# Second column pair of the MLP's down projection by seven products in four blocks of a layer instead of three

## The chip, the cores and the metric

The kernel runs on one core of a Trainium2 chip. Its engines work side by side, each with a queue of its own: TensorE (PE, with PEld for the load of its weights) multiplies matrices into PSUM banks, VectorE (DVE) and ScalarE (ACT) work element by element, GpSimd (POOL) and SyncE (SP) here mostly start transfers. Semaphores order them. The metric is the time of one execution in microseconds on the device, as a median of several runs; three runs of the kernel before gave 2193.33 (2192.96 to 2195.0).

## What is computed

A trunk of two decoder layers on 256 tokens of width 2048 in float32. Each layer normalises, runs an attention mixer (two head types in layer 0, sparse attention in layer 1) and adds the result, then normalises again and runs an MLP. The change is in the MLP alone:

```python
def sq_relu_mlp(h, w_up, w_down):
    return jnp.square(jax.nn.relu(h @ w_up)) @ w_down      # 2048 -> 8192 -> 2048

for layer in range(DEPTH):                                 # DEPTH = 2
    hn = rms_norm(h, ln_mix_g[layer])
    h = h + mixer(hn)                                      # even or odd
    hn = rms_norm(h, ln_mlp_g[layer])
    h = h + sq_relu_mlp(hn, w_mlp_up[layer], w_mlp_down[layer])
```

## The kernel before

**Products in three parts.** Every float32 product is made of three matmuls: both operands are split into a high part (a rounded copy, by ScalarE, line 280) and a low part (the value minus the copy, by VectorE, line 283), and high x high, high x low and low x high are summed in PSUM. A weight therefore costs a transfer, a ScalarE copy and a VectorE subtraction before TensorE can use it.

**Units.** The work of TensorE is one list of units, written in `units`; `run` (line 291) walks it. A unit has 1024 columns of weights to split. The split of a unit is issued while TensorE's unit three places ahead of it is issued, and there are four buffers (`wh`, `wl`) for split weights, so ScalarE can begin a split only when TensorE has finished the unit four places back. A plain unit (`a_units`, line 339) has 12 matmuls of 512 columns, lines 366 to 368 and 379. A unit of a seven-product pair has 6, lines 989 to 991.

**The MLP.** The 8192 hidden columns are cut into eight blocks of 1024. `up_units(b)` makes block b of the hidden layer with 16 plain units (two halves g of 512 columns, eight units each). Then comes a chain of small steps for each half: out of PSUM by transposes (line 443), turned over partitions by DMAs (line 449), relu and square on ScalarE, and split into high and low parts in `big` (lines 908 and 910). There is one place for the hidden parts of blocks 0 to 6, so block b may be written only when all of block b - 1 has been used (`used`, line 1010).

**The down projection of a block** has four column blocks of 512, taken as two pairs: c = 0 (columns 0 to 1023) and c = 1 (1024 to 2047). A plain pair (`pair_units`, line 1057) has 8 plain units. A pair by seven products (`seven_units`, line 937) has the tokens, the hidden rows and the columns cut in two each and makes the 2x2 by 2x2 block product with seven products in place of eight: x0, z0, x1, y0, x2, y1, x3, in this order, each of two units (a and b here). For this it needs sums of weights and sums of tokens:

- Sums of weights are made in four stage buffers of 1 MB (`Stage`, line 215). A stage is loaded by SP (line 229) or made from another one by an addition: on VectorE for x1, x2 and x3 (line 239, two halves of 1024 columns each), by a DMA that POOL starts and that adds as it writes for y1 (line 237). A VectorE addition is issued four units after the split that frees its place, or at the latest with the split that needs it.
- Sums of tokens are made once per block by `token_sums` (line 918): four rounds of a VectorE operation (line 929), a ScalarE copy (932) and a VectorE operation (934). They start when the sums of the block before have been used (`passed`, "sums") and when both hidden halves are there. x1, y0, x2 and y1 use them.

x0, z0 and x3 use the hidden parts themselves. The results of six of the seven products are added to the residual `xs` at once (line 1000); z0's product stays in a bank over the blocks and is added at the last block that has one (`ends`).

`WIDE = (1, 3, 5)` says in which blocks the second pair goes by seven products too. The first pair does in blocks 0 to 6; block 7 is plain throughout. So a layer has ten such pairs.

**What sets the order.** The list of units is written by hand: after the 16 units of `up_units(0)` come groups (the loop at line 1074), in each of which the units of the seven-product pairs are woven into plain units at the places `at`: `mine[0], others[0], mine[1]`, then the other plain units up to the next place. A spacing of one means one plain unit between the two units of a product and none behind them; a spacing of two, one more behind. The groups before:

| group | plain units | seven-product units |
| --- | --- | --- |
| 1 | up 1, pair c = 1 of block 0 (24) | block 0 c = 0 (14) |
| 2 | up 2, up 3, pair of block 2 (40) | block 1 c = 0 and 1, block 2 c = 0 (42) |
| 3 | up 4, up 5, pair of block 4 (40) | block 3 c = 0 and 1, block 4 c = 0 (42) |
| 4 | up 6, up 7, pair of block 6 (40) | block 5 c = 0 and 1, block 6 c = 0 (42) |

In groups 2 to 4 the spacing is two but for four places: z0 to x1 in all three pairs, and y0 to x2 in the second. Block 7's 16 plain units end the layer.

The chains of small steps (hidden parts, token sums) are generators that `Background` hands out: after every three matmuls comes a slot (line 331), in which up to two waiting steps are issued; a step says by `yield` how many slots the next one must wait. Where a unit needs the result of a chain that isn't done, `need` (line 143) runs slots until it is, so that all remaining steps are issued at once ahead of that unit. A unit of 12 matmuls has four slots, one of 6 has two.

Of the kernel before, what the change touches and what calls it, by code (L numbers as in the profile page):

```python
# [148 lines left out]
def trunk_kernel(ctx: ExitStack, tc: tile.TileContext, x, w_up, w_down, even_w_in, even_w_out,  # L149
# [303 lines left out]
    class Norm:  # L453
# [83 lines left out]
        def need(self, ks):  # L537
            if self is norms[0] and max(ks) < 2:
                return
            for n in {k // 4 for k in ks}:  # L540
                bg.need(self.tasks[n])
# [327 lines left out]
    def mlp(layer, norm, nxt):  # L869
        up, down = w_up[layer], w_down[layer]  # L870
        NBLK = DFF // 1024
        WIDE = (1, 3, 5)

        def hid(b):


            return big[:, 0:8] if b < NBLK - 1 else big[:, 8:16]
# [59 lines left out]
        def seven_units(b, c):  # L937

            def w(r, n):
                at = c * 1024 + n * 512
                return down[b * 1024 + r * 512:b * 1024 + r * 512 + 512, at:at + 512].rearrange("(k p) c -> p k c", p=128)

            turn = len(kept)
            places = summed + [smw[:, 0:2048]]
            bx, by, bz, bw = (places[(i - turn) % 4] for i in range(4))
            old = kept.get(turn - 1)
            final = c == 1 or b not in WIDE

            def gone(f):

                return f if turn else lambda i: current[0] >= start[0] and all(t.done for t in norm.tasks.values())

            x0 = Stage(bx, gone(lambda i: old["x1"].have[i] and old["y1"].have[i]), src=w(0, 0))
            z0 = Stage(bz, gone(lambda i: old["y1"].used[i]), src=w(1, 0))
            w0 = Stage(bw, gone(lambda i: old["z0"].used[i] and old["x3"].have[i]), src=w(0, 1))
            y0 = Stage(by, gone(lambda i: old["x3"].used[i]), src=w(1, 1))
            x1 = Stage(bx, lambda i: x0.used[i] and w0.have[i], add=w0.buf, prev=x0)
            x2 = Stage(bx, lambda i: x1.used[i] and y0.have[i], add=by, prev=x1)  # L960
            y1 = Stage(by, lambda i: y0.used[i] and x2.have[i] and w0.have[i], add=w0.buf, prev=y0, far=True)
            x3 = Stage(bx, lambda i: x2.used[i] and z0.have[i], add=bz, prev=x2)
            kept[turn] = dict(x1=x1, x3=x3, y1=y1, z0=z0)

            def hx(j0, half):
                return lambda j, part: hid(b)[:, j0 + j, part, half * 128:half * 128 + 128]

            def sx(i):
                return lambda j, part: xsum[:, part, i, j]

            h0 = lambda: [heads["hid", b, 0]]
            hd = lambda: [heads["hid", b, g] for g in range(2)]
            sm = lambda: [heads["sum", layer, b]]
            P, Q, R = bank[0], bank[1 + 2 * c], bank[2]
            ends = b == (NBLK - 2, WIDE[-1])[c]
            out_ = []

            for n, (st, lhs, need, o, new, half, col, neg) in enumerate((
                    (x0, hx(0, 0), h0, P, True, 0, 0, 0), (z0, hx(4, 0), hd, Q, b == c, 0, 0, 0),
                    (x1, sx(0), sm, R, True, 1, 1, 0), (y0, sx(3), sm, R, False, 0, 1, 0),  # L980
                    (x2, sx(1), sm, P, False, 0, 1, 1), (y1, sx(2), sm, P, False, 1, 1, 1),
                    (x3, hx(4, 1), hd, P, False, 1, 0, 0))):
                for i in range(2):
                    def gen(u, n=n, i=i, lhs=lhs, need=need, o=o, new=new, half=half, col=col, neg=neg):
                        bg.need(*need())
                        h, lo = (t[u % NHL].rearrange("p (j c) -> p j c", j=2) for t in (wh, wl))
                        for j in range(2):
                            jj = 2 * i + j
                            nc.tensor.matmul(o, lhs(jj, 0), h[:, j], start=new and jj == 0, stop=False, skip_group_check=True)  # L989
                            nc.tensor.matmul(o, lhs(jj, 0), lo[:, j], start=False, stop=False, skip_group_check=True)  # L990
                            nc.tensor.matmul(o, lhs(jj, 1), h[:, j], start=False, stop=jj == 3 and (n != 1 or ends), skip_group_check=True)  # L991
                            if jj == 3 and n == 0 and c == 1:
                                passed.add(("low", b))
                            if jj == 3 and (n != 1 or ends):
                                at = (2 * c + col) * 512
                                xd = xs[:, half, at:at + 512]
                                f = 2 * neg + half
                                if b == 0 and n == 0:
                                    bg.need(norm.rtask)
                                nc.vector.scalar_tensor_tensor(xd, o, norm.r2[:, f:f + 1], xd, op0=ALU.mult, op1=ALU.add)  # L1000
                                if final:
                                    passed.update({("sums", b)} if n == 5 else {("seven", b)} if n == 6 else ())
                            yield

                    out_.append((st, i * 1024, 1024, gen, True))
            return out_
# [3 lines left out]
        def used(b, g):  # L1010
# [3 lines left out]
            if b == NBLK - 1:  # L1014
                return ("sums", b - 1) in passed
            need_ = {("low", b - 1)} if g == 0 else {("seven", b - 1)} if b - 1 in WIDE else {("seven", b - 1), ("eight", b - 1)}
            return need_ <= passed
# [4 lines left out]
        def taken(f, *a):  # L1022
            at = len(units)
            f(*a)
            got = units[at:]
            del units[at:]
            return got
# [43 lines left out]

        start[0] = len(units) + 5
        up_units(0)
        for b in (1, *range(2, NBLK, 2)):
            if b > 1:
                plain_ = taken(up_units, b) + taken(up_units, b + 1) + taken(pair_units, b)
                seven = seven_units(b - 1, 0) + seven_units(b - 1, 1) + seven_units(b, 0)
            else:
                plain_ = taken(up_units, b) + taken(pair_units, b - 1)
                seven = seven_units(b - 1, 0)  # L1080


            m = len(seven) // 2
            if b == 1:
                at = [1, 7, 10, 13, 16, 19, 22]
            else:
                at = [2]
                for i in range(m - 1):
                    at.append(at[-1] + (1 if i in (1, 8, 10, 15) else 2))
            units.extend(plain_[:at[0]])  # L1090
            for i, (a, e) in enumerate(zip(at, at[1:] + [len(plain_)])):
                mine, others = seven[2 * i:2 * i + 2], plain_[a:e]
                units.extend([mine[0], others[0], mine[1]] + others[1:])
# [5 lines left out]

    out_proj(even_w_out, even_ready, norms[1], [(n, a, a + 8) for a in (0, 8) for n in range(NB)], 3)  # L1100
    mlp(0, norms[1], norms[2])


# [226 lines left out]

    out_proj(odd_w_out, odd_ready, norms[3], [(n, 0, 8) for n in range(NB)] + [(n, a, a + 4) for a in (8, 12) for n in range(3)] + [(3, 8, 16)], 0)
    mlp(1, norms[3], None)
    run()

# [52 lines left out]
```

## Time and profile before

| what | value |
| --- | --- |
| median of three runs | 2193.33 us |
| profiled execution, its own time | 2191.8 us |
| its span | 2190.0 us |
| granted clock of TensorE | 1.000 |
| busy: PE, PEld, DVE, ACT | 100%, 83%, 77%, 57% |
| HBM read | 410.52 MB |

The span is that of the instructions of one execution; its time is 1.8 us longer. A busy TensorE says little by itself, because neighbouring matmuls overlap; the waits of TensorE and the chain of work that ended last show whether it sets the time. Row form in the timeline: start in us, duration in us, engine, line, operation, written tile <- read tiles, shape, count, and in brackets the idle time ahead of it with what ended it. Layer 0's MLP lies between 442.5 and 1112.5 us of the span; layer 1's MLP is the last 670 us.

### The profile page before, as it was taken

To read this page: it belongs to the slowest core of one execution; us is meant where nothing else is said; L and a number is where in the kernel's file an instruction comes from. 1 tells how busy PE (TensorE), PEld (TensorE's weight loads), DVE (VectorE), ACT (ScalarE), POOL (GpSimd) and SP (SyncE) were. 2 spreads that over 40 slices of the span, in tenths; PEclk is the share of its full clock that TensorE was granted. 3 is DMA by queue.
4 is the path that set the end of the run, shared out by engine and by line. 5 is a ranking of instruction groups with operands and counts; after the bars stand their busy time and mean duration, and the time that the engine had idled before them with its cause. 6 is when DMAs were issued, how large, how long until landed. Compare 5 with 4: busy or idle time off the path is not lost.

```text
span 2190.0 us, 27524 instructions
## 1 busy us (share of the span) xinstructions
PE 2183.5 (100%) x9965; PEld 1808.6 (83%) x9965; DVE 1695.2 (77%) x2241; ACT 1243.7 (57%) x1563; POOL 76.4 (3%) x68
## 2 busy tenths in 40 slices
PE   9999999999999999999999999999999999999999
PEld 7788888888888888888888888888888888888887
DVE  5676766668989989989764676766689899899895
ACT  5555555455556656656643556555455665665663
POOL 0000000000000000000000000000000000000000
PEclk9999999999999999999999999999999999999999
DMA  7655656587677777777666664535776867867864
GB/s 271 193 190 172 191 187 202 173 285 217 216 239 233 230 243 224 241 240 225 193 196 198 223 197 136 161 109 178 244 241 180 282 203 219 280 198 232 269 203 154
DMA packets 287751, 463.73 MB, mean 212 GB/s; under 512 B 25344, under 2 KB 81920, under 8 KB 287616
## 3 DMA queue, kind: packets, MB, share of 16 engines
q1 hardware_dynamic: 280848, 439.89, 61.2%
q0 software_dynamic: 5760, 20.97, 5.2%
q8 instruction: 78, 1.28, 0.2%
q10 hardware_dynamic: 1008, 1.12, 0.2%
q14 instruction: 57, 0.47, 0.1%
HBM read 410.52 MB, written 2.10 MB: 188 GB/s over the span
## 4 chain that ended last, share of the span: by engine, by line
PE 97%; DVE 2%; DMA 1%; ACT 0%; issue 0%; SPq 0%; POOL 0%; DVEq 0%; ACTq 0%
PE bank L379 48%; PE bank L366 8%; PE bank L368 8%; PE bank L367 8%; PE bank L990 6%; PE bank L991 6%; PE bank L989 6%; PE bank L691 1%; PE bank L723 1%; PE bank L718 1%; PE bank L399 1%; DVE wl L283 1%; PE bank L400 1%; PE bank L398 1%; PE bank L1161 0%; DMA raw<-in_odd_w_in 0%
## 5 line engine op out<-in xcount | busy, mean ns | idle before, releaser
L283 DVE TENSOR_TENSOR wl<-raw,wh 128x1024 fp32r<-128x1024 f32 (+2 forms) x611 | 741.4, 1217 | 308.4 <-ACT wh L280 304.8
L280 ACT ACTIVATE wh<-raw 128x1024 fp32r<-128x1024 f32 (+2 forms) x611 | 642.8, 1056 | 555.0 <-PE bank L379 316.5
L379 PE MATMUL bank<-wh,xT 128*128 128x512 f32 x2592 | 733.4, 391 | 0.0
L379 PEld LDWEIGHTS bank<-wh,xT 128*128 128x128 f32 x2592 | 485.1, 188 | 99.1
L379 PE MATMUL bank<-wl,xT 128*128 128x512 f32 x1296 | 406.4, 391 | 0.1
L379 PEld LDWEIGHTS bank<-wl,xT 128*128 128x128 f32 x1296 | 243.2, 188 | 51.0 <-DVE wl L283 0.5
L280 ACT ACTIVATE wh<-sum 128x1024 fp32r<-128x1024 f32 x208 | 219.9, 1058 | 92.7 <-PE bank L379 50.3
L283 DVE TENSOR_TENSOR wl<-sum,wh 128x1024 fp32r<-128x1024 f32 x208 | 253.5, 1220 | 19.2 <-ACT wh L280 16.4
L990 PE MATMUL bank<-wl,big 128*128 128x512 f32 x560 | 218.0, 389 | 0.1
L989 PE MATMUL bank<-wh,big 128*128 128x512 f32 x560 | 217.9, 389 | 0.0
L991 PE MATMUL bank<-wh,big 128*128 128x512 f32 x560 | 217.8, 389 | 0.0
L366 PE MATMUL bank<-wh,xT 128*128 128x512 f32 x432 | 170.6, 395 | 0.0
L379 PE MATMUL bank<-wh,big 128*128 128x512 f32 x592 | 169.5, 392 | 0.0
L368 PE MATMUL bank<-wh,xT 128*128 128x512 f32 x432 | 168.3, 390 | 0.0
L367 PE MATMUL bank<-wl,xT 128*128 128x512 f32 x432 | 168.1, 389 | 0.0
L366 PE MATMUL bank<-wh,big 128*128 128x512 f32 x344 | 138.1, 401 | 0.0
L368 PE MATMUL bank<-wh,big 128*128 128x512 f32 x344 | 134.2, 390 | 0.0
L367 PE MATMUL bank<-wl,big 128*128 128x512 f32 x344 | 134.0, 390 | 0.0
L379 PEld LDWEIGHTS bank<-wh,big 128*128 128x128 f32 x592 | 110.9, 188 | 22.5
L990 PEld LDWEIGHTS bank<-wl,big 128*128 128x128 f32 x560 | 105.1, 188 | 22.5 <-DVE wl L283 0.7
L989 PEld LDWEIGHTS bank<-wh,big 128*128 128x128 f32 x560 | 105.1, 188 | 21.8
L991 PEld LDWEIGHTS bank<-wh,big 128*128 128x128 f32 x560 | 105.1, 188 | 21.7
(226 smaller groups left out, 2367.1 us busy)
## 6 DMA issues: line engine op xcount, KB each, us to landing
raw<-in_w_up SPq DMA_DIRECT2D x128, 1024.0 KB, 7.4
sum<-in_w_down SPq DMA_DIRECT2D x60, 1024.0 KB, 8.8
raw<-in_even_w_in SPq DMA_DIRECT2D x48, 1024.0 KB, 5.2
raw<-in_w_down SPq DMA_DIRECT2D x48, 1024.0 KB, 5.9
raw<-in_odd_w_in SPq DMA_DIRECT2D x40, 1024.0 KB, 5.2
sm<-in_w_down SPq DMA_DIRECT2D x20, 1024.0 KB, 7.5
t<-t SPq DMA_DIRECT2D x608, 32.0 KB, 3.3
raw<-in_even_w_out SPq DMA_DIRECT2D x16, 1024.0 KB, 5.2
```

Of the source, the lines that this page charges most:

```text
L280: nc.scalar.activation(h[:, at], r[:, at], AF.Copy)
L283: nc.vector.tensor_tensor(lo[:, at], r[:, at], h[:, at], ALU.subtract)
L366: nc.tensor.matmul(o, lhs(k, 0, hf), h[:, n], start=st, stop=False)
L367: nc.tensor.matmul(o, lhs(k, 0, hf), lo[:, n], start=False, stop=False)
L368: nc.tensor.matmul(o, lhs(k, 1, hf), h[:, n], start=False, stop=last and n == len(ks) - 1)
L379: nc.tensor.matmul(bks[hf], lhs(k, part, hf), w_[:, n], start=False, stop=False)
L398: nc.tensor.matmul(o, lhs(k, 0, hf), h[:, at], start=k == 0, stop=False)
L399: nc.tensor.matmul(o, lhs(k, 0, hf), lo[:, at], start=False, stop=False)
L400: nc.tensor.matmul(o, lhs(k, 1, hf), h[:, at], start=False, stop=k == KT - 1)
L989: nc.tensor.matmul(o, lhs(jj, 0), h[:, j], start=new and jj == 0, stop=False, skip_group_check=True)
L990: nc.tensor.matmul(o, lhs(jj, 0), lo[:, j], start=False, stop=False, skip_group_check=True)
L991: nc.tensor.matmul(o, lhs(jj, 1), h[:, j], start=False, stop=jj == 3 and (n != 1 or ends), skip_group_check=True)
```

## The change

`WIDE` becomes `(0, 2, 4, 5)`: the second pair goes by seven products in blocks 0, 2, 4 and 5, and is plain in blocks 1, 3 and 6. A layer has eleven pairs by seven products instead of ten, and three plain pairs instead of four, ahead of block 7. The bank of z0 is started at block 0 in both column pairs (`b == 0` instead of `b == c`).

The loop over groups is written anew, with three groups:

| group | plain units | seven-product units |
| --- | --- | --- |
| 1 | up 1, up 2, pair of block 1 (40) | block 0 c = 0 and 1, block 1 c = 0 (42) |
| 2 | up 3, up 4, pair of block 3 (40) | block 2 c = 0 and 1, block 3 c = 0 (42) |
| 3 | up 5, up 6, up 7, pair of block 6 (56) | block 4 c = 0 and 1, block 5 c = 0 and 1, block 6 c = 0 (70) |

The places now follow one rule: as many spacings of one as are needed for the plain units to suffice (`few`: 7, 4 and 16), given first to z0 to x1, then to y0 to x2, then x0 to z0, then x1 to y0. In group 1 the first two products keep the places 1 and 7, and x1 of block 0 follows at place 8 (10 before). In group 3 z0 to x1, y0 to x2 and x0 to z0 get a spacing of one in all five pairs, and x1 to y0 in the first.

```diff
-        WIDE = (1, 3, 5)
+        WIDE = (0, 2, 4, 5)
...
-                    (x0, hx(0, 0), h0, P, True, 0, 0, 0), (z0, hx(4, 0), hd, Q, b == c, 0, 0, 0),
+                    (x0, hx(0, 0), h0, P, True, 0, 0, 0), (z0, hx(4, 0), hd, Q, b == 0, 0, 0, 0),
...
-        for b in (1, *range(2, NBLK, 2)):
-            if b > 1:
-                plain_ = taken(up_units, b) + taken(up_units, b + 1) + taken(pair_units, b)
-                seven = seven_units(b - 1, 0) + seven_units(b - 1, 1) + seven_units(b, 0)
-            else:
-                plain_ = taken(up_units, b) + taken(pair_units, b - 1)
-                seven = seven_units(b - 1, 0)
+        for ups, pair, pairs in (((1, 2), 1, ((0, 0), (0, 1), (1, 0))), ((3, 4), 3, ((2, 0), (2, 1), (3, 0))),
+                                 ((5, 6, 7), 6, ((4, 0), (4, 1), (5, 0), (5, 1), (6, 0)))):
+            plain_ = [u for b in ups for u in taken(up_units, b)] + taken(pair_units, pair)
+            seven = [u for b, c in pairs for u in seven_units(b, c)]
             m = len(seven) // 2
-            if b == 1:
-                at = [1, 7, 10, 13, 16, 19, 22]
-            else:
-                at = [2]
-                for i in range(m - 1):
-                    at.append(at[-1] + (1 if i in (1, 8, 10, 15) else 2))
+            at = [1, 7] if ups[0] == 1 else [2]
+
+            few = m * 2 - len(at) * 2 + 2 + at[-1] - len(plain_)
+            ones = sorted(range(len(at) - 1, m), key=lambda i: ((1, 3, 0, 2, 6, 5, 4).index(i % 7), i))[:few]
+            for i in range(len(at) - 1, m - 1):
+                at.append(at[-1] + (1 if i in ones else 2))
             units.extend(plain_[:at[0]])
```

## The prediction, made before the result was known

> **What bounds the kernel now.** I read the page's busy shares, granted clock and chain first, then what TensorE waited for.
>
> ```profile
> span 2190.0 us, 27524 instructions
> ...
> PE 2183.5 (100%) x9965; PEld 1808.6 (83%) x9965; DVE 1695.2 (77%) x2241; ACT 1243.7 (57%) x1563; POOL 76.4 (3%) x68
> ...
> PEclk9999999999999999999999999999999999999999
> ...
> PE 97%; DVE 2%; DMA 1%; ACT 0%; issue 0%; SPq 0%; POOL 0%; DVEq 0%; ACTq 0%
> ```
>
> ```profile
> PE bank L203 <- DVE sq L199: 1.5, 1, 1.5
> PE bank L398 <- ACT wh L280: 0.6, 1, 0.6
> PE bank L399 <- DVE wl L283: 0.5, 1, 0.5
> ```
>
> TensorE is on the path almost everywhere, at full clock, and waits 2.6 us in all, at the start. A matmul less therefore shortens the span by its whole pitch, and a split that comes late lengthens it. Next come layer 0's MLP stretches (columns: us; busy us of PE, PEld, DVE, ACT, POOL; clock; DMA share; GB/s). The first is the group with one pair by seven products, the other the third group of three pairs.
>
> ```profile
> 486.90:571.30 84.40, 84.40 (x374) 69.84 (x373) 71.04 (x73) 48.60 (x50) 1.93 (x2) 1.00 0.78 248
> ...
> 903.10:1069.00 165.90, 165.90 (x734) 137.37 (x733) 151.28 (x153) 103.02 (x103) 5.23 (x6) 1.00 0.73 227
> ```
>
> VectorE is the runner-up: 151.28 of 165.9 us, 91%. What counts is how far ahead of TensorE it runs. So I took the tightest place that repeats, in layer 1: x1 of block 4's first pair. First VectorE, then two TensorE rows: x1's first matmul and its first use of the low part.
>
> ```profile
> 1919.41 1.23 DVE L283 TENSOR_TENSOR wl<-raw,wh 128x1024 fp32r<-128x1024 f32 x1 [1.11 <-ACT wh L280]
> 1920.55 0.75 DVE L1000 SCALAR_TENSOR_TENSOR xs<-bank,r_m,xs 128x512 f32<-128x512 f32 x1
> 1921.21 0.68 DVE L934 TENSOR_TENSOR big<-sq,big 128x512 fp32r<-128x512 f32 x1
> 1921.81 1.22 DVE L910 TENSOR_TENSOR big<-t,big 128x1024 fp32r<-128x1024 f32 x1
> 1922.95 1.22 DVE L283 TENSOR_TENSOR wl<-sum,wh 128x1024 fp32r<-128x1024 f32 x1
> 1924.08 0.69 DVE L929 TENSOR_TENSOR sq<-t,sq 128x512 f32<-128x512 f32 x1
> 1924.68 1.22 DVE L283 TENSOR_TENSOR wl<-raw,wh 128x1024 fp32r<-128x1024 f32 x1
> 1925.82 1.22 DVE L239 TENSOR_TENSOR sum<-sum,sum 128x1024 f32<-128x1024 f32 x1
> 1926.95 0.68 DVE L934 TENSOR_TENSOR big<-sq,big 128x512 fp32r<-128x512 f32 x1
> 1927.56 1.22 DVE L283 TENSOR_TENSOR wl<-sum,wh 128x1024 fp32r<-128x1024 f32 x1
> 1928.69 0.68 DVE L929 TENSOR_TENSOR sq<-t 128x512 f32<-128x512 f32 x1
> 1929.30 1.22 DVE L283 TENSOR_TENSOR wl<-raw,wh 128x1024 fp32r<-128x1024 f32 x1
> 1930.43 0.74 DVE L1000 SCALAR_TENSOR_TENSOR xs<-bank,r_m,xs 128x512 f32<-128x512 f32 x1
> 1931.09 1.22 DVE L239 TENSOR_TENSOR sum<-sum,sum 128x1024 f32<-128x1024 f32 x1
> 1932.22 1.22 DVE L283 TENSOR_TENSOR wl<-sum,wh 128x1024 fp32r<-128x1024 f32 x1
> 1933.36 0.68 DVE L934 TENSOR_TENSOR big<-sq,big 128x512 fp32r<-128x512 f32 x1
> 1933.96 1.22 DVE L283 TENSOR_TENSOR wl<-sum,wh 128x1024 fp32r<-128x1024 f32 x1
> ```
>
> ```profile
> 1935.74 0.39 PE L989 MATMUL bank<-wh,big 128*128 128x512 f32 x1
> 1935.96 0.39 PE L990 MATMUL bank<-wl,big 128*128 128x512 f32 x1
> ```
>
> From 1919.41 on VectorE has no idle time. x1's split ends at 1933.96 + 1.22 = 1935.18; it is used at 1935.96. **The lead is 0.78 us.** The spacing of starts gives what each operation costs the queue: 1.135 us for a split, a stage add (L239) or a hidden low part (L910), 0.66 for an addition to xs (L1000), 0.60 for a piece of the token sums (L929, L934). Check: 7 splits, 2 adds, 1 hidden part, 2 xs and 5 pieces make 7.95 + 2.27 + 1.135 + 1.32 + 3.0 = 15.7 us; less the last split that is 14.5, and 1919.41 + 14.5 is the 1933.96 at which that split starts.
>
> **The saving.** One plain unit takes
>
> ```profile
> 1042.60 2.72 PE bank L379 x12
> ```
>
> so a matmul has a pitch of 2.72/12 = 0.227 us. A plain pair has 8 units of 12 matmuls, 96; seven products have 14 units of 6, 84. One more pair of a layer by seven products saves 12 matmuls, 2.72 us; two layers 5.44 us. The flag for the bank (start at block 0) and the end at block 5 add no instruction.
>
> **What is added, and its cover.** For a layer: 6 more splits and 6 stage adds on VectorE (12 x 1.135), 2 more additions to xs (6 against 4; 1.3 us), 14.9 us in all; 6 ScalarE copies; 2 POOL additions by DMA. The weights are 4 MB either way, four issues on SP's queue instead of four, but each pair's first stage load now waits there for the POOL additions of the pair ahead, with the raw loads behind it. All this lies beside matmuls: VectorE has 165.9 - 151.3 = 14.6 us free in a group of three pairs. With the cover gone it would cost 14.9 us a layer. The additions by DMA land in
>
> ```profile
> DMA to landing us min/median/max: 4.9/6.6/10.3
> ```
>
> and the new order leaves block 4's first pair the least time for them: by the operations counted below issued 7 us before ScalarE would read the result and 14 us before TensorE needs it, so even 10.3 us is covered. I take nothing for it; the far end, 10.3 + 2.2 for the split against 14, is nothing too. The y0 to x2 spacing elsewhere is that of block 1's second pair now.
>
> **What is moved: the leads.** Seven units now lie closer: the last group weaves 70 of them among 56 plain units instead of 42 among 40. Which plain units go missing between them decides. At a pair's start x3b, p, x0a, p, x0b, p, z0a, p, z0b, x1a is the order quoted above (p a plain unit, a and b the halves of a product's unit); in the last group it is x3b, p, x0a, p, x0b, z0a, p, z0b, x1a. One plain unit less gives VectorE 2.72 us less, and takes 1.135 of work away. The lead thus shrinks by 1.6, and the lead was 0.78.
>
> *Block 5's first pair.* Helper steps are handed out after every three matmuls (a slot). Counting the yields, the sums of block b start 41 slots after its last up unit. Block 5's last up unit ends 60 slots ahead of x1a, and sums take 28 slots, so they run late: four pieces fall into the stretch ahead of x1a, the rest are forced at x1a. The output of block 6's first half (two transposes) falls in too, where before it came behind x1a:
>
> ```profile
> 1945.18 1.31 DVE L443 STREAM_TRANSPOSE t<-bank 128x512 f32<-128x512 f32 x2
> 1946.41 1.19 DVE L283 TENSOR_TENSOR wl<-raw,wh 128x1024 fp32r<-128x1024 f32 x1
> ```
>
> They cost 1.23 us. The stretch is then 6 splits 6.81, 2 xs 1.32, 4 pieces 2.40, hidden part 1.135, 2 adds 2.27, transposes 1.23: 15.2 us; and a ScalarE copy of a sum stands ahead of z0a's copy, for about 0.6 us of VectorE idle. 15.8 in all. Time to be had: 1935.96 - 1919.41 = 16.55, less 2.72: 13.8. **TensorE waits about 2.0 us at x1a.** Behind it come 3 splits (3.4), the four pieces left (2.4), and one turn DVE, ScalarE, DVE of the forced ones:
>
> ```profile
> 1929.41 0.63 ACT L932 ACTIVATE big<-sq 128x512 fp32r<-128x512 f32 x1 [1.87 <-DVE sq L929]
> ```
>
> 0.63 with its signals 0.75: 6.6 us, against 5.65 of TensorE time up to the next but one plain unit: another 0.9. Together 2.9 us. Late next are the splits of y0 and x2, with some 0.2 us of lead by the same count; then two plain units between neighbours let VectorE recover.
>
> *Block 6's first pair.* Sums start in time, as in the quoted stretch. Up to x1a 6 splits, 2 xs, 4 pieces, hidden part, 2 adds: 13.9 against 13.8; the next piece and plain split add 1.7 against 1.4 of matmuls. Late by 0.55 in all with 0.1 for a signal.
>
> *Block 4's first pair* has four close spacings in a row, but five plain units in a row ahead of it; by the same count 0.35 us of lead is left. Nothing.
>
> *Block 0's first pair.* x1a comes 40 slots after the up units instead of 48, and the sums, which start at slot 26, are forced there with two turns over ScalarE still to do. VectorE's earliest split goes by
>
> ```profile
> 1939.82 0.39 PE L989 MATMUL bank<-wh,big 128*128 128x512 f32 x1
> 1940.02 1.06 ACT L280 ACTIVATE wh<-raw 128x1024 fp32r<-128x1024 f32 x1 [1.66 <-PE bank L379]
> 1941.11 1.23 DVE L283 TENSOR_TENSOR wl<-raw,wh 128x1024 fp32r<-128x1024 f32 x1 [0.26 <-ACT wh L280]
> ```
>
> the end of the unit four places back (1939.82), to VectorE free again at 1941.11 + 1.135: 2.45 us. Then 4 pieces 2.4, two turns 1.4, the split 1.1: 7.4 in all against 7.25 of matmuls: late by 0.3 with the signal.
>
> The second pairs of blocks 0, 4 and 5 have no sums beside them; by the count they keep a lead of 2 us. Blocks 1 to 3 keep the spacing of now at x1.
>
> **Sum.** Waits 2.9 + 0.55 + 0.3 = 3.75 a layer, 7.5 in two; saved 5.44; net +2.1 us. The profiled execution has a span of 2190.0 and a time of 2191.8, 1.5 below the median 2193.33. By the profiled one 2193.9, by the median **2195.4 us**.
>
> No run shows a late split, so I bound the waits. Low end: none, the whole 5.44 saved, 2187.9. High end: operations cost their whole duration, 1.22, not 1.135 (the rival below), 2204. I take the spacing, since in the quoted stretch it holds for seventeen operations running.
>
> **The rivals.**
>
> *The whole gain.* If the sums are spread otherwise than by my count, or the queue runs further ahead at the start of these stretches, nothing waits: 2193.33 - 5.44 = 2187.9. For it: VectorE is 91% busy, not 100%. Against it: leads of 0.78 us in a schedule looser by a plain unit.
>
> *Slower: VectorE loses the overlap of neighbours.* Place: the same four stretches, where splits, sums and adds wait on signals of three engines. Price: 1.22 - 1.135 = 0.085 us for each operation of 1024 columns. Some 18 of them in block 5's stretch up to x2 cost 1.5, some 14 in block 6's 1.2, block 0's 0.8, block 4's 0.7 beyond its lead: 3.75 + 4.2 = 7.95 a layer, 15.9 in two, less 5.44: +10.5, 2203.8. From about a quarter of that on (1.2 us a layer more than my sum) the kernel is slower by over 0.2%. Against it: the rows have no such loss without an idle mark. [...]
>
> **How the numbers follow.** A measurement here tells about 0.2% (4.4 us) from no change. My forecast, part of the gain eaten and no difference to be told (2189 to 2197.7), has 0.53; the whole gain 0.22; slower 0.25, most of it by less than the full 10.5. The range reaches from the whole gain to half way into the slower rival: 2187.5 to 2200.5. Faster 0.22, same 0.53, slower 0.25.
>
> **What would show it.** The waits of TensorE should name VectorE's split (L283) some four to eight times a layer, about 3 to 4 us in sum, most of it at x1 and the two plain units behind it in block 5's first pair, and little in block 6's and 0's; 24 matmuls fewer; VectorE without idle time there. No such waits and a span near 2184.6 would prove the whole gain. Waits on a DMA, or waits in the second pairs too, would prove the sum wrong.

## The result

The kernel after took 2222.22 us (median of four runs, 2219.17 to 2224.91) against 2194.16 of the kernel before beside it: a ratio of 1.0126, interval 1.0115 to 1.0138. It is slower by some 28 us; the prediction said 2195.4, and its range ended at 2200.5.

The profiled execution took 2222.08 us with a span of 2220.3, 30.3 above the span before. The page of the kernel after, its span, its busy shares and the chain of work that ended last:

```profile
span 2220.3 us, 27555 instructions
...
PE 2186.9 (98%) x9941; PEld 1801.3 (81%) x9941; DVE 1721.5 (78%) x2269; ACT 1252.9 (56%) x1575; POOL 79.7 (4%) x72
...
PE 72%; DVE 11%; issue 7%; DMA 6%; SPq 2%; ACT 1%; POOL 0%; DVEq 0%; ACTq 0%; POOLq 0%
```

TensorE has 9941 matmuls, 24 fewer than 9965, so the change does what it says. But VectorE now holds 11% of the chain, where it held 2%. TensorE's waits after (us in total, times, longest):

```profile
PE bank L989 <- DVE xs L1000: 15.1, 10, 2.5
PE bank L379 <- DVE wl L283: 4.7, 5, 1.1
PE bank L990 <- DVE wl L283: 4.5, 4, 1.2
PE bank L989 <- ACT wh L280: 1.1, 1, 1.1
```

Before, none of these was there. The second and third line, 9.2 us, are the late splits that I had expected, at 7.5. **The first line I had not expected at all**: 15.1 us in which the first matmul of a product (L989) waits for an addition to the residual (L1000). The fourth line is one more wait of that kind under another name, that of y1 in block 2's second pair of layer 0. VectorE's row and then TensorE's:

```profile
752.25 0.74 DVE L1000 SCALAR_TENSOR_TENSOR xs<-bank,r_m,xs 128x512 f32<-128x512 f32 x1
...
753.14 0.47 PE L989 MATMUL bank<-wh,big 128*128 128x512 f32 x1 [1.10 <-ACT wh L280]
```

The addition (of x2's product, in the bank that y1 is summed in) ends at 752.99, and y1 starts 0.15 us later, the distance of all these waits. The copy that the profile names ended last, at 753.14, but it copies loaded weights, and y1 uses summed ones.

How long the seven-product stretch of a layer takes is seen from the first and last start of its first matmul, here for layer 1. The profile's rows for that line, the kernel before and then after:

```profile
L989 PE MATMUL bank<-wh,big x280: 389/389/389, 1563.1 to 2139.1; 128*128 128x512 f32 x140
```

```profile
L989 PE MATMUL bank<-wh,big x308: 388/389/470, 1579.6 to 2169.3; 128*128 128x512 f32 x154
```

That is 576.0 us before and 589.7 after, +13.7. Layer 0's rows go from 489.8 to 1066.2 and from 490.1 to 1081.1, 576.4 and 591.0: +14.6. Together these are 28.3 of the 30.3 us. (Most of the rest, 1.6, lies between the layers.) With the 5.44 us saved, TensorE must have lost 33.7 us in these stretches. I took all starts of matmuls in them and noted each step that exceeds the pitch of 0.227 us by over 0.1. Layer 0 / layer 1, in us:

| place | late splits | waits for an addition | predicted, a layer |
| --- | --- | --- | --- |
| block 0, first pair | 1.31 / 1.22 | 1.76 / 1.75 | 0.3 |
| block 2, second pair | - | 1.26 / - | 0 |
| block 4, first pair | 1.38 / 1.41 | 2.63 / 2.67 | 0 |
| block 4, second pair | 0.21 / 0.22 | 0.63 / 0.62 | 0 |
| block 5, first pair | 2.95 / 2.95 | 1.76 / 1.76 | 2.9 |
| block 5, second pair | - | 0.25 / 0.25 | 0 |
| block 6, first pair | 0.72 / 0.72 | 1.54 / 1.58 | 0.55 |
| sum | 6.6 / 6.5 | 9.8 / 8.6 | 3.75 |

Both layers together 31.5; the other 2.2 us are steps too small for the list. (This is more than the 25.4 us of the four lines above, which count from the end of the matmul ahead, 0.39 us after its start, and not from its pitch.) In the first pairs and in block 4's second pair the addition waited for is that of x1, and y0 waits; in the second pairs of blocks 2 and 5 it is that of x2, and y1 waits.

**Where a wait comes from.** Block 5's first pair, layer 1. VectorE's timeline after, with x1's addition last:

```profile
2036.44 1.22 DVE L283 TENSOR_TENSOR wl<-raw,wh 128x1024 fp32r<-128x1024 f32 x1
2037.57 1.22 DVE L239 TENSOR_TENSOR sum<-sum,sum 128x1024 f32<-128x1024 f32 x1
2038.71 1.22 DVE L283 TENSOR_TENSOR wl<-sum,wh 128x1024 fp32r<-128x1024 f32 x1
2039.84 1.22 DVE L283 TENSOR_TENSOR wl<-raw,wh 128x1024 fp32r<-128x1024 f32 x1
2040.98 0.74 DVE L1000 SCALAR_TENSOR_TENSOR xs<-bank,r_m,xs 128x512 f32<-128x512 f32 x1
```

TensorE's timeline beside it, from x1a to y0a:

```profile
2028.89 0.39 PE L989 MATMUL bank<-wh,big 128*128 128x512 f32 x1
2030.51 0.50 PE L990 MATMUL bank<-wl,big 128*128 128x512 f32 x1 [1.23 <-DVE wl L283]
...
2036.03 0.61 PE L379 MATMUL bank<-wh,xT 128*128 128x512 f32 x2
2037.71 0.73 PE L379 MATMUL bank<-wl,xT 128*128 128x512 f32 x2 [1.07 <-DVE wl L283]
...
2041.87 0.47 PE L989 MATMUL bank<-wh,big 128*128 128x512 f32 x1 [1.60 <-DVE xs L1000]
```

At 2030.51 and 2037.71 a split is late, where the prediction had put it: x1a and the next but one plain unit. The third wait is new. x1's product is complete with its last matmul just ahead of 2036.03, but y0 is summed in the same bank, so VectorE must have read the bank first. VectorE does so 5 us later: the addition stands behind the splits in its queue, the last of them (2039.84) that of the unit three places ahead. It ends at 2041.72, and y0a starts at 2041.87.

The same place in block 4's first pair before, VectorE and then TensorE, shows that this was close all along:

```profile
1942.26 0.74 DVE L1000 SCALAR_TENSOR_TENSOR xs<-bank,r_m,xs 128x512 f32<-128x512 f32 x1
...
1943.90 0.39 PE L989 MATMUL bank<-wh,big 128*128 128x512 f32 x1
```

The prediction quotes the rows ahead of it: x1b starts at 1939.82; only then is the buffer for the next split free; ScalarE copies (1940.02), VectorE subtracts (1941.11), and then comes the addition, which ends at 1943.00. x1b ends at 1941.18, the start 1939.82 and six pitches. So even with VectorE idle beforehand the bank comes free 1.82 us after x1b. With a plain unit between (a spacing of two) y0a starts 2.72 after it: **a margin of 0.9 us. With a spacing of one there is none, and y0 must wait for some 1.8 us.** The change gives block 4's first pair just that spacing, and elsewhere makes VectorE late by more than 0.9.

### The profile page after: what moved, and what is told of

It is laid out like the page before. It is cut to its first block, busy times and chain, and to the rows that moved or that the text cites. A ratio compares the mean times of both kernels' runs of the same rounds, so it can differ in the third digit from the quotient of the medians.

```text
span 2220.3 us, 27555 instructions
## 1 busy us (share of the span) xinstructions
PE 2186.9 (98%) x9941; PEld 1801.3 (81%) x9941; DVE 1721.5 (78%) x2269; ACT 1252.9 (56%) x1575; POOL 79.7 (4%) x72
## 4 chain that ended last, share of the span: by engine, by line
PE 72%; DVE 11%; issue 7%; DMA 6%; SPq 2%; ACT 1%; POOL 0%; DVEq 0%; ACTq 0%; POOLq 0%
PE bank L379 35%; PE bank L366 5%; DVE wl L283 5%; PE bank L368 5%; PE bank L367 5%; PE bank L989 5%; PE bank L990 5%; PE bank L991 5%; DMA raw<-in_w_up 2%; SPq L449 2%; DVE sum L239 1%; DMA sum<-in_w_down 1%; DMA raw<-in_odd_w_in 1%; ACT wh L280 1%; PE bank L691 1%
## 5 line engine op out<-in xcount | busy, mean ns | idle before, releaser
L283 DVE TENSOR_TENSOR wl<-raw,wh 128x1024 fp32r<-128x1024 f32 (+1 forms) x595 | 721.0, 1215 | 291.0 <-ACT wh L280 286.1
L280 ACT ACTIVATE wh<-raw 128x1024 fp32r<-128x1024 f32 (+1 forms) x595 | 625.6, 1055 | 527.8 <-PE bank L379 285.0
L379 PE MATMUL bank<-wh,xT 128*128 128x512 f32 x2592 | 734.0, 391 | 0.0
L379 PEld LDWEIGHTS bank<-wh,xT 128*128 128x128 f32 x2592 | 485.1, 188 | 99.5
L379 PE MATMUL bank<-wl,xT 128*128 128x512 f32 x1296 | 407.4, 392 | 4.7 <-DVE wl L283 4.7
L280 ACT ACTIVATE wh<-sum 128x1024 fp32r<-128x1024 f32 x228 | 240.0, 1056 | 116.1 <-PE bank L368 29.8
L283 DVE TENSOR_TENSOR wl<-sum,wh 128x1024 fp32r<-128x1024 f32 x228 | 277.0, 1217 | 30.4 <-ACT wh L280 29.0
L379 PEld LDWEIGHTS bank<-wl,xT 128*128 128x128 f32 x1296 | 242.5, 188 | 58.1 <-DVE wl L283 8.4
L989 PE MATMUL bank<-wh,big 128*128 128x512 f32 x616 | 240.9, 391 | 16.4 <-DVE xs L1000 15.1
L990 PE MATMUL bank<-wl,big 128*128 128x512 f32 x616 | 240.7, 391 | 4.7 <-DVE wl L283 4.5
L989 PEld LDWEIGHTS bank<-wh,big 128*128 128x128 f32 x616 | 115.6, 188 | 45.9 <-ACT wh L280 11.5
L379 PE MATMUL bank<-wh,big 128*128 128x512 f32 x528 | 151.2, 392 | 0.0
L990 PEld LDWEIGHTS bank<-wl,big 128*128 128x128 f32 x616 | 115.7, 188 | 31.1 <-DVE wl L283 7.9
L991 PEld LDWEIGHTS bank<-wh,big 128*128 128x128 f32 x616 | 115.6, 188 | 23.8
L367 PE MATMUL bank<-wl,big 128*128 128x512 f32 x312 | 121.6, 390 | 0.0
L379 PEld LDWEIGHTS bank<-wh,big 128*128 128x128 f32 x528 | 98.9, 188 | 20.1
```

The lines of the kernel that those rows point to most:

```text
L280: nc.scalar.activation(h[:, at], r[:, at], AF.Copy)
L283: nc.vector.tensor_tensor(lo[:, at], r[:, at], h[:, at], ALU.subtract)
L367: nc.tensor.matmul(o, lhs(k, 0, hf), lo[:, n], start=False, stop=False)
L379: nc.tensor.matmul(bks[hf], lhs(k, part, hf), w_[:, n], start=False, stop=False)
```

## The experiments

My theory (A in some expectations) was: the 15 us are the wait for x1's bank behind VectorE's queue. The rivals: VectorE is short of time as a whole, so the wait only shows where the shortage falls, and freeing the bank would let the next split be late instead (B); or its late splits are one disturbance, and all else follows.

### x1's addition left out, and x0's as a control

Each leaves out the additions to the residual of one product (so that product is missing from the sum), 22 operations of VectorE.

```diff
+                                if n != 2:      # in the control: n != 0
-                                nc.vector.scalar_tensor_tensor(xd, o, ...)
+                                    nc.vector.scalar_tensor_tensor(xd, o, ...)
```

> The changed kernel without the addition of x1's product to the residual (11 a layer left out, 0.66 us of VectorE each; its bank is not read at x1's end). Theory A, bank behind the queue: y0 goes into x1's bank and has to wait until VectorE has read it, and VectorE's addition stands behind the split three places ahead. Then the 10 waits of TensorE on L1000 (15.1 us) go, the time falls by about 17 us to some 2205. Rival B, VectorE has too much work and the wait's name only says where it shows: each of the five tight places a layer gains 0.66 us, the time falls by about 6.6 us to some 2215, and the waits come back at the next split. Rival C, weights land late: no change, 2222.

> The changed kernel without the addition of x0's product to the residual: as many operations of the same length as in the run without x1's addition, but no product waits for this one. Theory A: the waits on L1000 at y0 stay (some 15 us), only the late splits of x1 lose up to 0.66 us each: about 5 us less, 2217. Rival B: the same gain as without x1's addition, 2215. Rival C: no change, 2222.

Without x1's addition: 2208.68, ratio 1.0067 (1.0047 to 1.0087), span 2207.2. Without x0's: 2212.24, ratio 1.0083 (1.0063 to 1.0103), span 2213.0. TensorE's waits without x1's addition, and then without x0's:

```profile
PE bank L379 <- DVE wl L283: 7.0, 8, 1.4
PE bank L990 <- DVE wl L283: 4.8, 6, 1.2
PE bank L989 <- DVE xs L1001: 1.3, 1, 1.3
```

```profile
PE bank L989 <- DVE xs L1001: 13.1, 8, 2.0
PE bank L379 <- DVE wl L283: 4.4, 6, 1.1
PE bank L990 <- DVE wl L283: 1.1, 2, 0.6
```

The two save VectorE the same work, and their intervals overlap, so the times alone don't decide. The waits do. Without x1's addition the wait for the bank falls from 15.1 to 1.3, but late splits rise from 9.2 (L379 and L990) to 11.8. Without x0's the bank wait stays, at 13.1, and late splits fall to 5.5. With the wait on ScalarE's copy (1.1 after and without x1's addition, none without x0's) the listed waits fall from 25.4 to 14.2 and to 18.6. Both theories have a share: the bank is a cause of its own, but a queue shorter by the same amount helps more than half as much. Neither theory's forecasts fit: A had 2205 and 2217, B 2215 twice, and the control gained more than either gave it. It may gain almost as much as the other: in the execution profiled, of 2214.79 us, TensorE ran twice at half clock for some 3.4 us (see the last section), and the control's other run took 2209.69.

### The addition ahead of the split

The split of the unit three places ahead is issued behind x1's addition, not before it. Nothing is left out.

```diff
-            for _ in gen(u):
+            for hold in gen(u):
                 bg.slot(2 if u < NT else ROOM)
-                next(rest, None)
+                if not hold:
+                    next(rest, None)
...
-                            yield
+                            yield n == 2 and i == 1 and j == 0
```

> The changed kernel with all its work; in x1's second unit the split three places ahead is issued behind the addition to the residual instead of ahead of it. Theory A: every wait at y0 shrinks by one split, 1.135 us (1.75, 2.67, 0.62, 1.76, 1.58 become 0.6, 1.5, 0, 0.6, 0.45 in a layer), the late splits stay: about 10 us less in two layers, 2212. Rival B: the same work in another order gains nothing, 2222. Rival C: no change, 2222.

2210.45, ratio 1.0079 (1.0059 to 1.0098), span 2206.3. Block 5's first pair in this kernel, VectorE and then TensorE (y0a):

```profile
2027.04 1.22 DVE L283 TENSOR_TENSOR wl<-sum,wh 128x1024 fp32r<-128x1024 f32 x1
2028.17 0.74 DVE L1001 SCALAR_TENSOR_TENSOR xs<-bank,r_m,xs 128x512 f32<-128x512 f32 x1
...
2029.07 0.47 PE L990 MATMUL bank<-wh,big 128*128 128x512 f32 x1 [0.44 <-DVE xs L1001]
```

One split less stands ahead of the addition, and y0's wait falls by the 1.135 us of a split, to 0.6 in blocks 0 and 5 (0.44 by the mark), 1.4 in block 4 and 0.44 in block 6, as expected. The queue order alone is thus worth some 12 us of time, and rival B, which gave another order nothing, does not fit. The rest remains: by the list of waits 8.3 us of late splits (9.2 before) and 6.6 us of waits for a bank, 1.2 of which stand under a copy's name again.

### The token sums on GpSimd

```diff
-                nc.vector.tensor_tensor(d, a, c, op)
+                nc.gpsimd.tensor_tensor(d, a, c, op)
...
-                nc.vector.tensor_tensor(lo, dst, h, ALU.subtract)
+                nc.gpsimd.tensor_tensor(lo, dst, h, ALU.subtract)
```

> The changed kernel with the eight pieces of the token sums of each block on GpSimd instead of VectorE (4.8 us a block less on VectorE, at the tight places). Theory A and rival B both: late splits go, and with them most of the waits on L1000, since VectorE has its lead back; some 25 of the 31 us, 2197 or less. If GpSimd slows VectorE down beside it, or its pieces come too late for x1, the gain is smaller or none: then VectorE's splits beside GpSimd's pieces are longer than 1.22 us, or TensorE waits on GpSimd. Rival C: no change, 2222.

2236.06, ratio 1.0195 (1.0175 to 1.0214): worse than the kernel after. VectorE's groups, splits of summed weights, first in the kernel after, then with the sums on GpSimd:

```profile
L283 DVE TENSOR_TENSOR wl<-sum,wh 128x1024 fp32r<-128x1024 f32 x228 | 277.0, 1217 | 30.4 <-ACT wh L280 29.0
```

```profile
L283 DVE TENSOR_TENSOR wl<-sum,wh 128x1024 fp32r<-128x1024 f32 x228 | 310.2, 1365 | 30.6 <-ACT wh L280 28.8
```

A piece of the sums mostly takes 1.3 to 2.3 us on GpSimd against 0.68 on VectorE. The mean of these splits, over the whole run, goes from 1.217 to 1.365 us; beside a piece one takes up to 2.3. GpSimd's rows and then VectorE's, in block 5's first pair of layer 1:

```profile
2040.34 1.46 POOL L934 TENSOR_TENSOR big<-sq,big 128x512 fp32r<-128x512 f32 x1 [0.74 <-ACT big L932]
2041.76 2.27 POOL L929 TENSOR_TENSOR sq<-t 128x512 f32<-128x512 f32 x1
```

```profile
2040.60 2.28 DVE L283 TENSOR_TENSOR wl<-sum,wh 128x1024 fp32r<-128x1024 f32 x1
2042.80 2.30 DVE L283 TENSOR_TENSOR wl<-raw,wh 128x1024 fp32r<-128x1024 f32 x1
```

Each of these splits ends 1.07 or 1.08 us behind the end of the piece beside it (2041.80 and 2044.03), as if it had waited for it; what holds it, no run shows. Over the run VectorE is busy with splits of 1024 columns for 1156.8 us instead of 1093.0, so it loses there most of the 67 us that 112 pieces of 0.60 would free. Its queue is hardly shorter, and this run can't tell the theories apart.

### Three blocks, in the new order

`WIDE = (0, 2, 4)`: ten pairs a layer as before, in the new order of blocks 0 to 3, with the last blocks woven loosely.

```diff
-        WIDE = (0, 2, 4, 5)
+        WIDE = (0, 2, 4)
...
-                                 ((5, 6, 7), 6, ((4, 0), (4, 1), (5, 0), (5, 1), (6, 0)))):
+                                 ((5, 6), 5, ((4, 0), (4, 1), (5, 0))), ((7,), 6, ((6, 0),))):
...
-            at = [1, 7] if ups[0] == 1 else [2]
+            at = [1, 7] if ups[0] == 1 else [2] if len(ups) == 2 else [2, 5, 8]
```

> Second pair by seven products in blocks 0, 2 and 4 alone, in the changed kernel's order: ten such pairs a layer as before the change, the first two groups as changed, then up 5, up 6 and the pair of block 5 with three pairs, and up 7 with the pair of block 6 around the last pair. The dense last group is undone, the changed first group stays. Theory A: TensorE has as many matmuls as before, and the waits of block 0 stay (1.2 late, 1.75 at y0, about 3 us a layer), the waits of blocks 4, 5 and 6 go: 2194 + 6 to 8 = 2200 to 2202. If the new first group were harmless, 2194; if the waits came from the order of the blocks and not from the close spacing, 2210 or more.

2203.75 (ten runs), ratio 1.0041 (1.0029 to 1.0053). TensorE's timeline, block 0's first pair in layer 1:

```profile
1604.52 0.73 PE L379 MATMUL bank<-wl,xT 128*128 128x512 f32 x2 [0.97 <-DVE wl L283]
...
1608.68 0.47 PE L989 MATMUL bank<-wh,big 128*128 128x512 f32 x1 [1.60 <-DVE xs L1000]
```

In this layer block 0's waits are those of the kernel after (0.95 and 1.59 there); in layer 0 the late split waits 1.85 us, and a window of 3.4 us behind it (525.58 to 528.99) has a granted clock of 0.50. In blocks 4 to 6 one wait for a bank is left, y1's in block 4's second pair, of 0.98 and 0.44 us. So the 28 us divide roughly: about 9.6 remain with ten pairs, in the new order that starts at block 0; some 18.5, net of the 5.44 saved, come with the eleventh pair and the close weaving of the last group.

### Other places for the wait to go

Three kernels moved spacings or steps. The first starts the last group one place sooner, so that block 4's x1 to y0 gets a spacing of two.

```diff
-            at = [1, 7] if ups[0] == 1 else [2]
+            at = [1, 7] if ups[0] == 1 else [2] if ups[0] == 3 else [1]
```

> The changed kernel with the last group begun one plain unit sooner, so that 15 close spacings suffice and the one between x1 and y0 of block 4 goes. Theory A: the wait at that y0 (2.63 and 2.67) falls by 1.4 or more, since a plain unit more lies between x1 and y0; the late split at block 4's x1 stays or grows by up to 1 us: 2222 less 1 to 4. Rival B: nothing but the sum of the work counts, 2222.

2222.55, ratio 1.0116 (1.0084 to 1.0148). Its waits:

```profile
PE bank L989 <- DVE xs L1000: 10.6, 10, 1.6
PE bank L379 <- DVE wl L283: 6.9, 6, 1.8
PE bank L990 <- DVE wl L283: 6.4, 6, 1.2
```

Block 4's bank wait falls from 2.65 to 0.54 us, but as much appears as late splits at x0, z0 and the plain unit behind: 4.1 us more in L379 and L990, most of it there. The wait moved, as rival B has it. The second lets the hidden part of block 5 be read sooner, so that its sums start sooner.

```diff
-                        yield 24 if b else 12
+                        yield 16 if b == 5 else 24 if b else 12
```

> The changed kernel with block 5's relu issued 16 slots after its turning DMAs instead of 24, so that its token sums start 5.4 us sooner and are done when x1 comes. Theory A, late splits from sums that run late: in block 5's first pair the late splits of x1 and of the plain units behind it fall from 1.39 + 1.23 to about 1 and the wait at y0 from 1.76 to about 0.8, some 5 us less in two layers, 2217. If the sums only move within a stretch that is full anyway: no change. If the DMAs have not landed by then, ScalarE waits on them and TensorE loses more.

2234.66, ratio 1.0171 (1.0138 to 1.0204). ScalarE's timeline and then TensorE's:

```profile
2020.66 1.06 ACT L899 ACTIVATE t<-t 128x1024 f32<-128x1024 f32 x1 [7.29 <-DMA t<-t]
...
2024.73 0.77 PE L989 MATMUL bank<-wh,big 128*128 128x512 f32 x1 [5.66 <-DVE xs L1000]
```

In block 5 the bank wait did fall, to 0.54, and one late split went. But ScalarE now reaches the turned block before its DMAs have landed, and holds the copies of all later splits for 7.3 us. The third kernel joined these two with the addition ahead of the split, and started block 0's second product at place 8.

```diff
-            at = [1, 7] if ups[0] == 1 else [2]
+            at = [1, 8] if ups[0] == 1 else [2] if ups[0] == 3 else [1]
```

> The changed kernel with x1's addition issued ahead of the split, the last group begun one plain unit sooner, block 5's sums sooner, and block 0's x1 one plain unit later. If the waits are independent the gains add up: 2222 less 12 (as measured), less 3, 5 and 2: 2200. It beats the kernel before (2194) only if the leads also win what is late behind them.

2233.4, ratio 1.0163 (1.0137 to 1.0188): the wait on the DMAs rules here too.

### x1's stage added by a DMA

VectorE no longer makes x1's sum of weights; a DMA that adds as it writes does, as for y1.

```diff
-            x1 = Stage(bx, lambda i: x0.used[i] and w0.have[i], add=w0.buf, prev=x0)
+            x1 = Stage(bx, lambda i: x0.used[i] and w0.have[i], add=w0.buf, prev=x0, far=True)
```

> The changed kernel with the two stage additions of x1 made by POOL's adding DMA, as those of y1 are, instead of by VectorE: 2.27 us less for VectorE in each pair, in the stretch ahead of x1. Theory A, VectorE's queue is too late at a few places: in blocks 4, 5 and 6 the late splits at x1 (1.3, 1.5, 0.4 us a layer) go, the waits at y0 (2.65, 1.76, 1.58) shrink by a half, block 0's (its additions lie long before) stay: from 15.5 to about 8 us a layer, 2222 to some 2207. If the transfers land too late (10.3 us at most, 10.9 us between the splits of x0 and x1), ScalarE waits on them and the time does not fall.

> The same, and x1's addition to the residual issued ahead of the split, block 0's x1 one plain unit later, the last group begun one plain unit sooner. By theory A some 4 to 5 us of waits a layer are left, 2196 to 2198; below 2.7 us a layer it beats the kernel before (2194).

> The kernel before with the stage additions of x1 by POOL's DMA. TensorE does not wait on VectorE there, so VectorE's 45 us less bring nothing: 2194, within 0.2%. If it is slower, these transfers cost something by themselves, by the raw loads that they delay, and that cost has to be taken off in the two runs with the changed kernel.

In the kernel after: 2222.14, ratio 1.0125 (1.0096 to 1.0155), no gain. With the addition ahead of the split and the looser starts (`at` as above): 2214.15, ratio 1.0082 (1.0059 to 1.0105). In the kernel before: 2198.13, ratio 1.0016 (1.0006 to 1.0025).

The late splits at x1 of blocks 4 to 6 go, as expected, but at block 0 of the kernel after z0 now waits twice for its hidden part (0.74 and 0.53 us in layer 1), and the late split behind x1 waits 1.84 where it waited 0.95. The waits at y0 shrink less than expected, to 1.97 us in block 4 and 1.7 in block 5, and in layer 1 new ones of 1.0 to 1.2 us come in the second pairs of blocks 4 and 5. The joined version misses its 2196 to 2198 by some 17 us; its list of waits has 6.8 us of late splits, 3.3 for banks and 3.5 for copies. In the kernel before the added DMA traffic costs 4 us by itself. The traces show where it stands. It starts one unit behind x0's splits, at 1573.82 and 1577.29 in layer 1 of the kernel after, together with the DMAs that turn the hidden block. SP then needs 13.02 us instead of 8.41 to start twelve of these, and ScalarE waits 6.42 us instead of 2.48 for a raw load among them. Ahead of z0 in block 4's second pair it waits 7.02 us for the load of a stage. Why these starts and loads take longer, no run shows.

### A shorter queue: no low parts of the token sums

The low parts of the token sums are not made, and the matmuls read the high part in their place: four pieces fewer a block on VectorE, at the places where the first pairs are late.

```diff
-                nc.vector.tensor_tensor(lo, dst, h, ALU.subtract)
...
-                return lambda j, part: xsum[:, part, i, j]
+                return lambda j, part: xsum[:, 0, i, j]
```

> The changed kernel without the low parts of the token sums (four VectorE pieces of 0.60 us a block left out; the matmuls use the high part twice, so their count stays). Theory A: late splits at x1 go in blocks 4 to 6 and 0, and y0 waits about 1 us less each: 15.5 to about 6 us a layer, 2203. If the sums do not matter, 2222.

2201.03 (eight runs), ratio 1.0025 (1.0013 to 1.0037). Its waits (lines are one less here), and then VectorE and TensorE at block 4's x1 to y0:

```profile
PE bank L988 <- DVE xs L999: 6.8, 7, 1.8
PE bank L379 <- DVE wl L283: 0.3, 1, 0.3
```

```profile
1918.61 1.22 DVE L283 TENSOR_TENSOR wl<-sm,wh 128x1024 fp32r<-128x1024 f32 x1 [0.54 <-ACT wh L280]
1919.75 0.74 DVE L999 SCALAR_TENSOR_TENSOR xs<-bank,r_m,xs 128x512 f32<-128x512 f32 x1
...
1920.64 0.47 PE L988 MATMUL bank<-wh,big 128*128 128x512 f32 x1 [1.81 <-DVE xs L999]
```

With 2.4 us less in VectorE's queue (four pieces of 0.6) the late splits are gone and the bank waits are less than half. One remains at full size where VectorE had been idle just before: block 4's, with its spacing of one. TensorE loses 1.97 us there (1.81 by the mark), as the 1.82 and a signal have it. That wait comes from the spacing, with no lateness of VectorE in it.

**What follows.** The loss has two parts that feed each other: VectorE is late by one to three microseconds in the first pairs, which costs late splits; and the same lateness counts again at y0, because x1's bank has only 0.9 us of margin, or none. No version beat the kernel before.

## Why the prediction was wrong

- **The saving** of 24 matmuls was right. At the pitch of 0.227 us they are 5.44 us; no run measures this by itself.
- **Block 5's first pair**: 2.9 predicted, 2.95 measured, and the eight pieces of the sums fall as counted, four ahead of x1a's split and four behind. But x1a took 1.6 of it and the next but one plain unit 1.3, where I had 2.0 and 0.9; that the sum agrees so closely is partly luck. **Block 6's**: 0.55 predicted, 0.72 measured. In these two places the count of VectorE's queue by its spacing holds for the splits.
- **The step that failed** is "Late next are the splits of y0 and x2, with some 0.2 us of lead". I asked of each split that it end before its own use, and nothing of the other work in the same queue. But x1's addition stands in it behind a split, and y0 waits for the bank that it frees. That term was missing in every first pair but those of blocks 1 to 3: 18.4 us in both layers with the second pairs, against nothing predicted. That is more than half of the 31.5 us. The late splits alone came to 13.1 us, against 7.5.
- **Block 4's "Nothing"** was wrong by 1.4 us of late splits. I let five plain units in a row build up a lead. In the list only three stand in a row there: the second half of x3 and the first of x0 part them from the other two. And weights came late, as rows of ScalarE and VectorE after show:

```profile
1908.06 2.01 ACT L280 ACTIVATE wh<-raw 128x1024 fp32r<-128x1024 f32 x2 [1.56 <-DMA raw<-in_w_up]
...
1909.15 1.23 DVE L283 TENSOR_TENSOR wl<-raw,wh 128x1024 fp32r<-128x1024 f32 x1 [1.40 <-ACT wh L280]
```

How much each of the two costs, no run separates.

- **Block 0** was late by 1.2 to 1.3, not 0.3, and not at x1a, whose split had 1.6 us of lead, but at the plain unit behind x1b, since the sums still due came behind x1a's split. VectorE was held ahead of it, for the DMAs that turn the hidden block; my count began with a queue that had caught up:

```profile
1593.24 1.23 DVE L897 SCALAR_TENSOR_TENSOR t<-t 128x1024 f32<-128x1024 f32 x1 [2.14 <-DMA t<-t]
```

The kernel before has the same idle time there (2.12 us ahead of 1576.79), and its looser places make up for it.

- **"By the count they keep a lead of 2 us"**, of the second pairs, does not hold. x1a's split ends 0.45 us ahead of its use in blocks 0 and 5 of the kernel after, and is late by 0.2 in block 4. For the banks there is no lead at all in blocks 4 and 5 (waits of 0.62 and 0.25 us).
- **"No run shows a late split"** overlooks one in the kernel before, in x1a of block 3's first pair of layer 0. VectorE's row and then TensorE's:

```profile
755.64 1.23 DVE L283 TENSOR_TENSOR wl<-sum,wh 128x1024 fp32r<-128x1024 f32 x1
...
756.92 0.50 PE L990 MATMUL bank<-wl,big 128*128 128x512 f32 x1
```

The split ends at 756.87, and TensorE loses 0.36 us. So the lead of 0.78 us that I took for the tightest was not the least.

- **The rival of lost overlap** was on the right side for another reason. VectorE's starts after still lie 1.135 apart (2036.44, 2037.57, 2038.71, 2039.84), so its price was not paid. The 1.22 us of these rows is again one operation's duration, and not its cost to the queue. **The whole gain** fell with the first waits.
- Of what I had named as proof against the sum, the waits in second pairs came. TensorE's list names no DMA; late transfers show only through ScalarE and VectorE, as in blocks 0 and 4.

## What to carry to other kernels

Where an engine works in order, a lead must be counted for everything in its queue that somebody waits for: not only the operand of the next product, but also the read that frees a bank for the product after it. Before products are moved closer, take from the trace how long after the last matmul of a bank it is read, and hold this against the gap to the bank's next use; here 1.82 against 2.72 us left 0.9, and a gap of nothing cost 2. An engine busy for 91% of a stretch may have no time at all in the one place where its work comes in a burst.

## What was not expected of the hardware

**TensorE's clock was halved after some waits of 2 us.** Without x0's addition, y0 waits at block 4 and the granted clock is 0.50 for the next 3.4 us (layer 1; in layer 0 the same follows a wait of 1.84). TensorE's timeline, and then the window behind it:

```profile
1931.52 0.64 PE L989 MATMUL bank<-wh,big 128*128 128x512 f32 x1 [2.02 <-DVE xs L1001]
```

```profile
1931.66:1935.06 3.40, 3.40 (x9) 2.64 (x10) 1.98 (x2) 0.67 (x1) 0.86 (x1) 0.50 1.05 234
```

At half the clock such a window loses some 1.7 us by my estimate (half of 3.4), about as much as the wait itself. A wait of 2.51 us in the kernel after left the clock at 1.00 (1918 to 1940), so it isn't the length alone that decides. With the sums sooner, 6.8 us at 0.50 (2021.70 to 2028.50) began within the wait of 5.66 us. What decides, no run shows.
